# S5 head: input matrices transposed ahead of the embedding's, the skip diagonal added on TensorE, taps loaded earlier, phase tables tied to the back rotation

## The chip, the cores and the metric

The kernel runs on one core of one Trainium2 chip. The time is the device time of one execution in microseconds (us); lower is better. The core has five engines that work at once, each through its own list of instructions strictly in order: TensorE (PE, with its weight loads shown apart as PEld), VectorE (DVE), ScalarE (ACT), GpSimd (POOL) and SyncE (SP). An engine waits at an instruction until what that instruction needs is ready, and what stands behind it in the list waits too. DMA transfers are issued from the lists of SP, ACT and POOL.

## The reference

A trunk of two layers works on 1024 positions of 1024 channels. Layer 0 mixes positions with an S5 state-space mixer, layer 1 with a short gated convolution. After each mixer come a dense SwiGLU network and a per-layer embedding that is gated by the residual; at the end stands one norm. Only the S5 mixer and the embedding's product matter here:

```
for i in range(DEPTH):
    hn = rmsnorm(h, norm_mix_g[i])
    mix = s5_mixer(hn, ...) if i % 2 == 0 else shortconv_mixer(hn, ...)
    h = h + mix
    h = h + swiglu_ffn(rmsnorm(h, norm_ffn_g[i]), ffn_w_in[i], ffn_w_out[i])
    gate = sigmoid(rmsnorm(h, norm_ple_g[i]) @ ple_w_gate[i])
    h = h + gate * (p[i] @ ple_w_up[i])

# s5_mixer, per group g of 16 channels (64 groups, 64 complex states each)
abar = exp(dt * a);  bb = (abar - 1) / a * b
state[t] = abar * state[t-1] + bb @ u[t]
y[t] = real(c @ state[t]) + d_skip * u[t]
z = gelu(y);  val, gate = split(z @ w_glu);  mix = val * sigmoid(gate)
```

## The kernel before

**S5.** The 64 groups are worked on in 8 lumps of 8 groups. A position is split into a block (128 blocks) and a place inside the block (8 places, `T`). Inside a block the recurrence is a small matrix: powers of `abar` times B and C give a kernel matrix `kp` (16 rows for each group, 8 lags of 16 channels), which DMAs spread into the block-Toeplitz matrix `M`. Across blocks the recurrence is a scan on VectorE. The state is turned by a phase table `E` first, so that the scan is real, and turned back after it.

One lump `b` goes through these steps, named as in the code:

- `gen_in(b)`: ScalarE writes the normed input into `raw`, TensorE transposes it, ScalarE copies it to `U`. B times powers is built on VectorE in `raw`, transposed, and copied by ScalarE to `wbt`.
- `states(b)`: eight matmuls `pb<-U,wbt` give the block states in PSUM (`pb`, one buffer).
- `phases(k)`: VectorE builds the phase table `ptab` (one buffer) of lumps 2k and 2k+1, by doubling, in 26 instructions. `gen_phase(b)` spreads one lump's part into `E` by four DMAs that stand in POOL's list (two buffers of `E`).
- `scan_turned(b)`: VectorE's `tmp<-pb,sgnA,E`. This is the first instruction of a lump's scan; it needs all of `pb` and of `E`. The result goes by two SP DMAs with halves swapped to `tw`.
- `scan_plain(b)`, `scan_run(b)`, `scan_back(b)`: the rest of the rotation, the scan into `gv`, the back rotation in place. The last instruction of the back rotation is kept as `done["back"]`.
- `gen_out(b)`: C times powers on VectorE (`W1`), then eight matmuls `pstr<-W,bbA` to PSUM, copied by ScalarE to `kp`. Then POOL multiplies the identity by the skip weights (`dd`) and adds it to the lag-0 part of `kp` (L1190).
- `gen_swap(b)`, `gen_toeplitz(b)`: SP DMAs that build the swapped C matrix and `M` from `kp`. For the last lump both go into rooms of `ulow`, which the embedding's split weights held before.
- `outputs(b)`, `channels(b)`: matmuls with `M`, `W1`, `W2`, GELU to `zt`, transposes, split into high and low parts.

**The embedding's product.** For each layer `l`, `up_split(l)` transposes `p` and copies the weight rows `wraw` through TensorE (a matmul with the identity) into two-part form in `ulow`, and `up_product(l)` makes 96 matmuls into `pstu`. Every six of these make one tile that ScalarE copies to `ev` (two buffers) and SP stores. Nothing needs the products before a layer's network has ended, so the 192 matmuls are spread between the S5's on TensorE, layer 0's first.

**What sets the order.** The program is written in the order of the calls; a scheduler with a timing model then sets each engine's list. It follows priorities (the embedding's copies rank ahead of and its matmuls behind the rest), the free buffers of the pools (three PSUM buffers `tr` for `pstr`, two `tu` for `pstu`, one `tx` for `pstx`), and explicit marks: `tc.issue_after(x)` lets nothing inside it be placed before instruction `x`. In the kernel before, `up_split(0)` is placed after the transposes of the S5's parameters (`turned`), and the convolution's taps `cw` (three DMAs in POOL's list) are placed after the clearing of `M` (`done["clear"]`).

After the S5 come the GLU's products from `glu` on, and then networks, convolution and norms, in the same order in both kernels but for small exchanges at the network's starts.

Of the kernel before, what the change touches and what calls it, by code (L numbers as in the profile page):

```python
# [9 lines left out]
F32 = mybir.dt.float32  # L10
# [4 lines left out]
ALU = mybir.AluOpType  # L15
# [3 lines left out]
P = 128  # L19
# [5 lines left out]
def trunk(  # L25
# [7 lines left out]
    nc = tc.nc  # L33
    V, A, G, PE = nc.vector, nc.scalar, nc.gpsimd, nc.tensor

    S, D = x.shape[1], x.shape[2]
    T = S // P
# [4 lines left out]
    PKT = PD // P  # L42
    NG, NP = s5_a_re.shape[1], s5_a_re.shape[2]
    KG = D // NG
# [12 lines left out]
    ident = const.tile([P, P], F32, name="ident")  # L57
# [32 lines left out]
    def split(hi, lo, src):  # L90
        A.copy(hi, src)  # L91
        V.tensor_tensor(lo, src, hi.bitcast(F32), ALU.subtract)  # L92
# [162 lines left out]
    done = {}  # L255
# [490 lines left out]
    def up_room(l, i, s):  # L746

        return ulow[:, i, l * 2 * D + s * D:l * 2 * D + (s + 1) * D]

    def up_split(l, raws):  # L750

        for b in range(2):
            sl = slice(b * 512, (b + 1) * 512)
            for kt in range(PKT):
                pt = psum(tr)
                transposes(pt, [raws[b][:, c, kt * P:(kt + 1) * P] for c in range(4)])
                split_pe(up_room(l, kt, 0)[:, sl], up_room(l, kt, 1)[:, sl], pt)
            for kt in range(PKT):
                pt = psum(tr)
                PE.matmul(pt, ident, raws[2 + kt][:, sl], start=True, stop=True)  # L760
                split_pe(up_room(l, PKT + kt, 0)[:, sl], up_room(l, PKT + kt, 1)[:, sl], pt)

    def up_product(l, mm_prio, ev_prio):
        for t in range(T):
            sl = slice(t * P, (t + 1) * P)
            for nb in range(2):
                cs = slice(nb * 512, (nb + 1) * 512)
                with tc.high_priority(offset=mm_prio):
                    ps = psum(tu)
                    for kt in range(PKT):  # L770
                        mm3(ps, up_room(l, kt, 0)[:, sl], up_room(l, kt, 1)[:, sl], up_room(l, PKT + kt, 0)[:, cs],
                            up_room(l, PKT + kt, 1)[:, cs], kt == 0, kt == PKT - 1)
                with tc.high_priority(offset=ev_prio):
                    ev = evp.tile([P, 512], F32, name="ev", tag="ev")
                    A.copy(ev, ps)
                    nc.sync.dma_start(out=updram[l][:, t, cs], in_=ev)
# [77 lines left out]
    GB = P // KG  # L854
    NBT = NG // GB
# [11 lines left out]
    gen = tc.alloc_tile_pool(name="s5g", bufs=1, side="right")  # L867
# [38 lines left out]


    ld_n = st.tile([NG, 1], F32, name="ld_n")
    nc.scalar.dma_start(out=ld_n, in_=s5_log_dt[0].unsqueeze(1))
    an = [st.tile([NG, 2, NP], F32, name=f"an{i}") for i in range(2)]  # L910
    for i, src in enumerate((s5_a_re, s5_a_im)):
        for r in range(2):
# [1 line left out]
    gn = st.tile([NG, KG], F32, name="gn")  # L914
# [3 lines left out]
    bn = st.tile([NG, 2, NP, KG], F32, name="bn")  # L918
    for r, src in enumerate((s5_b_re, s5_b_im)):
        nc.sync.dma_start(out=bn[:, r], in_=src[0])  # L920
    raws0 = up_load(0, (rawp, rawp, gen, gen), ("r0", "r1", "wbt", "tw"))
# [16 lines left out]
    turned = PE.transpose(pp[:, 2 * NG:3 * NG], dtb, ident[:NG, :NG]).ins  # L938
    are, aim, dt = (st.tile([P, NG], F32, name=f"prm{i}") for i in range(3))
    for i, tl in enumerate((are, aim, dt)):  # L940
        V.tensor_copy(tl, pp[:, i * NG:(i + 1) * NG])
    with tc.issue_after(turned):
        up_split(0, raws0)
    up_product(0, -1, -100)


    def swapped(dst, src, queue=nc.sync):
        for a, c in ((R0, R1), (R1, R0)):
            queue.dma_start(out=dst[a], in_=src[c])

    xbs = [st.tile([P, NG, KG], F32, name=f"xb{i}") for i in range(2)]
    cA, cS = (gen.tile([P, NG, KG], F32, name=f"cc{i}") for i in range(2))
    for hf in range(2):
        pt = psum(tr)
        for k in range(8):
            PE.transpose(pt[:, k * NG:(k + 1) * NG],
                         bn.rearrange("p a n k -> p (a n) k")[:, :, 8 * hf + k], ident[:NG, :NG])
        A.copy(xbs[0][:, :, 8 * hf:8 * hf + 8], pt.rearrange("p (k g) -> p g k", k=8))
    swapped(xbs[1], xbs[0], nc.scalar)
    for hf in range(2):  # L960
        pt = psum(tr)
        for b in range(4):
            PE.transpose(pt[:, b * P:(b + 1) * P], cn[:, 4 * hf + b].rearrange("p a n -> p (a n)"), ident)
        A.activation(cA[:, 32 * hf:32 * hf + 32].rearrange("p g k -> p (g k)"), pt, AF.Copy, scale=sgnA)
    swapped(cS, cA)

    gnb = st.tile([NG, T, KG], F32, name="gnb")
    G.tensor_copy(gnb, gn.unsqueeze(1).broadcast_to([NG, T, KG]))
    gk = gen.tile([P, NG], F32, name="gk")
    pg_ = psum(tr)  # L970
    PE.transpose(pg_[:, 0:NG], gnb.rearrange("p a n -> p (a n)"), ident[:NG, :NG])
# [1 line left out]
    dk = gen.tile([KG, NG], F32, name="dk")  # L973
# [134 lines left out]
    LB = 2  # L1108
    LQ = LB * HQ
    M = run.tile([P, GB, P], F32, name="M")  # L1110
    sv = run.tile([P, GB, P], F32, name="sv")
    gv = run.tile([P, GB, P], F32, name="gv")
    done["clear"] = G.memset(M, 0.0).ins
    G.memset(gv[:, :, 0:1], 0.0)

    def tmp_tile():
# [2 lines left out]
    def phases(lump):  # L1119
        pt = gen.tile([P, 2, LQ, NJ], F32, name="ptab", tag="ptab")  # L1120
        qs = slice(lump * LQ, (lump + 1) * LQ)
        V.memset(pt[:, 0, :, 0:1], 1.0)
        V.memset(pt[:, 1, :, 0:1], 0.0)
        for k in range(6):
            n = lo = 1 << k
            shp = [P, LQ, n]
            eb, fb = (ew[:, i, qs, k:k + 1].broadcast_to(shp) for i in range(2))
            v = gen.tile([P, LQ * NJ], F32, name="ph", tag="ph")[:, 0:2 * LQ * n]
            v = v.rearrange("p (i q n) -> p i q n", i=2, q=LQ)
            u = pt[:, :, :, lo:lo + n]  # L1130
            for o, w in ((v, fb), (u, eb)):
                tt(o, pt[:, :, :, 0:n], w.unsqueeze(1).broadcast_to([P, 2, LQ, n]), ALU.mult)
            tt(u[:, 0], u[:, 0], v[:, 1], ALU.subtract)
            tt(u[:, 1], u[:, 1], v[:, 0], ALU.add)
        ptabs[lump] = pt
# [4 lines left out]
    def gen_in(b):  # L1140
# [20 lines left out]
        for hf in range(2):  # L1161
# [4 lines left out]
                              start=i == 0, stop=i == 1, is_transpose=True)  # L1166
            A.copy(wbt[:, 4 * hf:4 * hf + 4].rearrange("p c n -> p (c n)"), pt)

    def gen_out(b):

        gsl = slice(b * GB, (b + 1) * GB)
        shp = [P, GB, NL, KG]
        W1 = Ws[b] = run.tile(shp, F32, name="W1", tag="W1", bufs=2)
        A.copy(W1[:, :, 0, :], cA[:, gsl])
        shp1 = [P, GB, T, KG]
        tm = tmp_tile()[:, 0:GB * P].rearrange("p (g s k) -> p g s k", g=GB, s=T)
        for o, pw, cc in ((W1[:, :, 1:NL, :], pwr, cA), (tm, pwn, cS)):
            tt(o, pw[:, gsl, 1:NL].unsqueeze(3).broadcast_to(shp1), cc[:, gsl].unsqueeze(2).broadcast_to(shp1), ALU.mult)
        tt(W1[:, :, 1:NL, :], W1[:, :, 1:NL, :], tm, ALU.subtract)
        kp = kps[b] = gen.tile([KG, GB, T, KG], F32, name="kp", tag="kp")  # L1180
        for hf in range(2):
            pk = psum(tr)
            for c in range(4):
                PE.matmul(pk[0:KG, c * P:(c + 1) * P], bbA[:, b * GB + 4 * hf + c, :], W1[:, 4 * hf + c, 0:T, :],
                          start=True, stop=True)
            A.copy(kp[:, 4 * hf:4 * hf + 4].rearrange("p g s k -> p (g s k)"), pk[0:KG, :])
        dd = gen.tile([KG, GB, KG], F32, name="dd", tag="dd")
        G.tensor_tensor(dd, ident[:KG, :KG].unsqueeze(1).broadcast_to([KG, GB, KG]),
                        dk[:, gsl].unsqueeze(2).broadcast_to([KG, GB, KG]), ALU.mult)
        G.tensor_tensor(kp[:, :, 0, :], kp[:, :, 0, :], dd, ALU.add)  # L1190

    def halves(a):
        return [a[:, hf * 4:hf * 4 + 4] for hf in range(2)]
# [82 lines left out]
    def channels(b, zt):  # L1276
        for hf in range(2):
# [2 lines left out]
            v = ulow.rearrange("p q (k l w j) -> p q k l w j", k=KT, l=2, w=2)  # L1280
            split_pe(v[:, :, b, 0, hf, :], v[:, :, b, 1, hf, :], pt, by_kt)

    phases(0)
    gen_in(0)
    states(0)
# [10 lines left out]
    for b in range(NBT):  # L1296
        nx, after = b + 1, b + 2
        if nx < NBT:
            gen_out(nx)
        scan_run(b)  # L1300
        if nx < NBT:
            scan_turned(nx)
        if nx == last:
            late = late_halves(0)
            for part in late:
                G.memset(part, 0.0)
            gen_swap(last, late_halves(2))
            gen_toeplitz(last, late)
        scan_back(b)
        if nx < NBT:  # L1310
            scan_plain(nx)
        if nx < last:
            phase = after % LB == 0
            if phase:
                phases(after // LB)
            zt = outputs(b)
            gen_swap(nx)
            gen_toeplitz(nx, [M])
            gen_phase(after)
            gen_in(after)  # L1320
            states(after)
            if after == last:
                glu_raws.extend(glu_load(0, u) for u in range(3))
            channels(b, zt)
        else:
            zt = outputs(b)
            if nx == last:
                channels(b, zt)
# [142 lines left out]
```

## Time and profile before

| what | value |
|---|---|
| median of the runs | 2272.39 us (3 runs, 2271.51 to 2277.5) |
| the profiled execution | 2272.43 us, span 2270.6 us |
| TensorE busy | 2174.3 us (96%) |
| VectorE busy | 1644.2 us (72%) |
| ScalarE busy | 914.3 us (40%) |
| GpSimd busy | 368.3 us (16%) |
| first scan instruction of lumps 0 to 7 | 60.63, 81.46, 102.17, 121.65, 140.90, 164.68, 183.06, 201.75 us |
| first matmul of the GLU's products | 228.44 us |

Times inside the execution are microseconds from the start of the span. A row of the timeline has the start, the duration of the run of like instructions, the engine, the line, the operation, output and inputs with their sizes, how many instructions, and in brackets how long the engine had been idle and what ended that. Fp32 matmuls appear as two records each. The part of the kernel that the change touches ends where the GLU's products start.

### The profile page before, as it was taken

The numbers are of one execution on the slowest core, as the hardware profiler recorded it, in microseconds if no ns is written. First come the engines' busy times: TensorE is split into PE (matmuls) and PEld (weight loads), VectorE is DVE, ScalarE is ACT, GpSimd is POOL, SyncE is SP. The second block draws the span as 40 slices with busy tenths as digits, with TensorE's granted clock in tenths as the row PEclk, the third lists the DMA queues.
The fourth block names the chain that finished last, engine by engine and source line by source line (L and its number), as shares of the span: only waits on it lengthen the run. The fifth ranks groups of instructions, "written<-read, shape, count | busy, mean of one in ns | idle before, by whom it ended". The sixth has DMA issues, their size and how long they took to land. (4 is left out here: it accounts for less than half of the span.)

```text
span 2270.6 us, 27968 instructions
## 1 busy us (share of the span) xinstructions
PE 2174.3 (96%) x10025; PEld 1788.0 (79%) x10025; DVE 1644.2 (72%) x2742; ACT 914.3 (40%) x1743; POOL 368.3 (16%) x441
## 2 busy tenths in 40 slices
PE   7977999899999999999979999989999999999998
PEld 5866888788888877878858888868888888787887
DVE  6786424977777787887587776398777777778864
ACT  7553422544444443344343332154444344333342
POOL 2121000011111112342010000110111111224310
PEclk9999999999999999999989999999999999999999
DMA  8635301344444468664232233633444545876613
GB/s 258 181 84 126 120 19 47 103 164 147 153 148 154 144 236 306 250 233 178 90 111 85 86 96 125 253 112 121 147 160 143 164 139 187 326 258 229 253 63 112
DMA packets 234186, 358.14 MB, mean 158 GB/s; under 512 B 23856, under 2 KB 166192, under 8 KB 234048
## 3 DMA queue, kind: packets, MB, share of 16 engines
q1 hardware_dynamic: 203056, 246.72, 33.3%
q0 software_dynamic: 30432, 109.08, 13.7%
q8 instruction: 79, 1.29, 0.2%
q10 hardware_dynamic: 560, 0.57, 0.1%
q14 instruction: 59, 0.48, 0.1%
HBM read 225.53 MB, written 114.29 MB: 150 GB/s over the span
## 5 line engine op out<-in xcount | busy, mean ns | idle before, releaser
L125 PE MATMUL psmm<-ulow,ws 128*128 128x512 f32 x896 | 353.0, 394 | 14.5 <-ACT ws L91 13.1
L127 PE MATMUL psmm<-ulow,ws 128*128 128x512 f32 x896 | 351.8, 393 | 3.2 <-DVE ws L92 3.2
L126 PE MATMUL psmm<-ulow,ws 128*128 128x512 f32 x896 | 352.5, 393 | 0.4 <-DVE ulow L92 0.4
L125 PE MATMUL psmm<-uhigh,ws 128*128 128x512 f32 x672 | 262.2, 390 | 2.9 <-DVE u L370 2.9
L127 PE MATMUL psmm<-uhigh,ws 128*128 128x512 f32 x672 | 261.8, 390 | 0.0
L126 PE MATMUL psmm<-uhigh,ws 128*128 128x512 f32 x672 | 261.8, 390 | 0.0
L91 ACT CAST ws<-raw 128x512 fp32r<-128x512 f32 x224 | 138.7, 623 | 275.0 <-PE psmm L127 265.6
L488 POOL DMA_DIRECT2D hw<-hs x154 | 116.0, 754 | 765.9 <-DVE hs L92 740.0
L125 PEld LDWEIGHTS psmm<-ulow,ws 128*128 128x128 f32 x896 | 170.2, 190 | 52.1 <-ACT ws L91 14.2
L127 PEld LDWEIGHTS psmm<-ulow,ws 128*128 128x128 f32 x896 | 169.9, 190 | 39.6 <-DVE ws L92 4.3
L126 PEld LDWEIGHTS psmm<-ulow,ws 128*128 128x128 f32 x896 | 170.3, 190 | 36.0 <-DVE ulow L92 0.7
L630 DVE TENSOR_TENSOR h<-psmm,h 128x512 f32<-128x512 f32 x234 | 155.4, 682 | 45.7 <-PE psmm L127 25.8
L639 POOL TENSOR_TENSOR h<-part,h 128x512 f32<-128x512 f32 x100 | 138.9, 1393 | 243.3 <-ACT part L638 215.1
L125 PE MATMUL psmm<-ulow,w 128*128 128x512 f32 x380 | 151.1, 398 | 14.0 <-DVE h L630 10.1
L92 DVE TENSOR_TENSOR ws<-raw,ws 128x512 fp32r<-128x512 f32 x224 | 153.6, 688 | 5.7 <-ACT ws L91 5.5
L125 PEld LDWEIGHTS psmm<-uhigh,ws 128*128 128x128 f32 x672 | 126.3, 188 | 29.9 <-issue 2.8
L126 PE MATMUL psmm<-ulow,w 128*128 128x512 f32 x380 | 148.4, 390 | 0.0
L127 PE MATMUL psmm<-ulow,w 128*128 128x512 f32 x380 | 148.3, 390 | 0.0
L127 PEld LDWEIGHTS psmm<-uhigh,ws 128*128 128x128 f32 x672 | 126.2, 188 | 26.2
L126 PEld LDWEIGHTS psmm<-uhigh,ws 128*128 128x128 f32 x672 | 126.2, 188 | 26.1
L91 ACT CAST ws<-st 128x512 fp32r<-128x512 f32 x168 | 103.8, 619 | 100.9 <-PE psmm L127 91.1
L125 PE MATMUL psmm<-w,ulow 128*128 128x512 f32 (+1 forms) x360 | 139.2, 387 | 0.0
(276 smaller groups left out, 4458.7 us busy)
## 6 DMA issues: line engine op xcount, KB each, us to landing
hw<-hs POOLq DMA_DIRECT2D x154, 512.0 KB, 4.2
w<-hw SPq DMA_DIRECT2D x88, 768.0 KB, 5.5
raw<-in_ffn_w_in_dram SPq DMA_DIRECT2D x88, 512.0 KB, 3.9
raw<-in_ffn_w_out_dram SPq DMA_DIRECT2D x44, 512.0 KB, 5.5
hd<-h POOLq DMA_DIRECT2D x24, 512.0 KB, 2.9
h<-hd SPq DMA_DIRECT2D x24, 512.0 KB, 5.8
raw<-in_conv_w_in_dram SPq DMA_DIRECT2D x24, 512.0 KB, 3.8
w<-hw SPq DMA_DIRECT2D x88, 128.0 KB, 5.4
```

Source lines behind the costliest of these rows:

```text
L91: A.copy(hi, src)
L92: V.tensor_tensor(lo, src, hi.bitcast(F32), ALU.subtract)
L125: PE.matmul(ps, ahi, bhi, start=start, stop=False, skip_group_check=more)
L126: PE.matmul(ps, ahi, blo, start=False, stop=False, skip_group_check=more)
L127: PE.matmul(ps, alo, bhi, start=False, stop=stop, skip_group_check=more)
L488: nc.gpsimd.dma_start(out=hidden[j][:, :, c].rearrange("q p l j -> p q l j"), in_=hs.bitcast(F32))
L630: done["sum"] = V.tensor_tensor(h[t][:, cs], ps, h[t][:, cs], ALU.add).ins
L639: G.tensor_tensor(h[t][:, cs], part, h[t][:, cs], ALU.add)
```

## The change

1. The load of the time steps (`ld_n`) goes from ScalarE's list to SP's.
2. The sixteen transposes of the S5's input matrices (`bn`), the two copies of them to `xb`, and the two DMAs that make the swapped copy stand ahead of `up_split(0)` and `up_product(0)`, which are now placed after the last of these transposes and after the last copy.
3. In `up_split(1)`, the part for layer 1, the weight rows are split straight from SBUF, by one ScalarE copy and one VectorE subtraction of 128 x 1024 for each of the two row blocks. The four matmuls with the identity, the four with the negated identity and the eight ScalarE copies of 512 columns behind them go.
4. The taps' DMAs are placed after the copy `gnb`, an early POOL instruction, where they waited for the clearing of `M`.
5. The skip diagonal `dd` of lump b+1 is made by POOL when lump b's output matrices are made, and is added by TensorE: eight matmuls of 16 columns per lump into the same PSUM tile. POOL's addition on `kp` goes.
6. `phases` of lumps 2, 4 and 6 is placed after the latest back rotation.

```
-            for kt in range(PKT):
+        for kt in range(PKT):
+            if l:
+                split(up_room(l, PKT + kt, 0), up_room(l, PKT + kt, 1), raws[2 + kt])
+                continue
+            for b in range(2):
+                sl = slice(b * 512, (b + 1) * 512)
                 pt = psum(tr)
                 PE.matmul(pt, ident, raws[2 + kt][:, sl], start=True, stop=True)
...
-    nc.scalar.dma_start(out=ld_n, in_=s5_log_dt[0].unsqueeze(1))
+    nc.sync.dma_start(out=ld_n, in_=s5_log_dt[0].unsqueeze(1))
...
-    with tc.issue_after(turned):
-        up_split(0, raws0)
-    up_product(0, -1, -100)
...
-            PE.transpose(pt[:, k * NG:(k + 1) * NG],
-                         bn.rearrange("p a n k -> p (a n) k")[:, :, 8 * hf + k], ident[:NG, :NG])
-        A.copy(xbs[0][:, :, 8 * hf:8 * hf + 8], pt.rearrange("p (k g) -> p g k", k=8))
+            turned = PE.transpose(pt[:, k * NG:(k + 1) * NG],
+                         bn.rearrange("p a n k -> p (a n) k")[:, :, 8 * hf + k], ident[:NG, :NG]).ins
+        done["xb"] = A.copy(xbs[0][:, :, 8 * hf:8 * hf + 8], pt.rearrange("p (k g) -> p g k", k=8)).ins
     swapped(xbs[1], xbs[0], nc.scalar)
+    with tc.issue_after(turned), tc.issue_after(done["xb"]):
+        up_split(0, raws0)
+    up_product(0, -1, -100)
...
-    G.tensor_copy(gnb, gn.unsqueeze(1).broadcast_to([NG, T, KG]))
+    done["clear"] = G.tensor_copy(gnb, gn.unsqueeze(1).broadcast_to([NG, T, KG])).ins
...
-    done["clear"] = G.memset(M, 0.0).ins
+    G.memset(M, 0.0)
...
+    dds = {}
+
+    def skip(b):
+        dds[b] = gen.tile([KG, GB, KG], F32, name="dd", tag="dd")
+        G.tensor_tensor(dds[b], ident[:KG, :KG].unsqueeze(1).broadcast_to([KG, GB, KG]),
+                        dk[:, b * GB:(b + 1) * GB].unsqueeze(2).broadcast_to([KG, GB, KG]), ALU.mult)
...
                 PE.matmul(pk[0:KG, c * P:(c + 1) * P], bbA[:, b * GB + 4 * hf + c, :], W1[:, 4 * hf + c, 0:T, :],
-                          start=True, stop=True)
+                          start=c == 0, stop=True, skip_group_check=c > 0)
+            for c in range(4):
+                PE.matmul(pk[0:KG, c * P:c * P + KG], ident[:KG, :KG], dds[b][:, 4 * hf + c, :], start=False, stop=True,
+                          skip_group_check=True)
             A.copy(kp[:, 4 * hf:4 * hf + 4].rearrange("p g s k -> p (g s k)"), pk[0:KG, :])
-        dd = gen.tile([KG, GB, KG], F32, name="dd", tag="dd")
-        G.tensor_tensor(dd, ident[:KG, :KG].unsqueeze(1).broadcast_to([KG, GB, KG]),
-                        dk[:, gsl].unsqueeze(2).broadcast_to([KG, GB, KG]), ALU.mult)
-        G.tensor_tensor(kp[:, :, 0, :], kp[:, :, 0, :], dd, ALU.add)
+        if b + 1 < NBT:
+            skip(b + 1)
...
+    skip(0)
     phases(0)
...
             if phase:
-                phases(after // LB)
+                with tc.issue_after(done["back"]):
+                    phases(after // LB)
```


The edits make the scheduler set other lists. Three places follow. The first is the head of TensorE's list; `praw` is the embedding's `p`, `bn` the S5's input matrices. Before:

```order
L937 MATMUL pstr<-ident,an_138 128x64
L937 MATMUL pstr<-ident,an_139 128x64
L938 MATMUL pstr<-ident,dtb 128x64
L287 MATMUL pstr<-ident,praw 128x128 x8
L293 MATMUL pstr<-ulow,identn 128x512 x2
L760 MATMUL pstr<-wraw,ident 128x512 x2
```

In the change:

```order
L942 MATMUL pstr<-ident,an_138 128x64
L942 MATMUL pstr<-ident,an_139 128x64
L943 MATMUL pstr<-ident,dtb 128x64
L958 MATMUL pstr<-ident,bn 128x64 x16
L287 MATMUL pstr<-ident,praw 128x128 x12
L293 MATMUL pstr<-ulow,identn 128x512 x3
```

The sixteen transposes of `bn` stand ahead of the embedding's first. The product's matmuls also stand elsewhere in TensorE's list. Ahead of lump 0's last `pb` matmul there were 78 of them and are now 48; between the last `pb` of lumps 0 and 1 there are 54 in both; between those of lumps 1 and 2 there were 39 and are 36; between those of lumps 2 and 3 there were 21 and are 48; the last 6 come behind that, where before none were left.

The second place is VectorE's list just ahead of lump 2's first scan instruction. Here `W_1288` is the `W1` buffer, `ptab` and `ph` belong to `phases(1)`. Before:

```order
L882 TENSOR_TENSOR sv<-sv,tw 128x8x127
L1251 SCALAR_TENSOR_TENSOR gv<-r_132,sv 128x127 x7
L882 TENSOR_TENSOR W_1288<-pwr,cc_424 128x8x128
L1251 SCALAR_TENSOR_TENSOR gv<-r_132,sv 128x127
L882 TENSOR_TENSOR W_1288<-W_1288,tmp 128x8x128
L886 SCALAR_TENSOR_TENSOR tmp<-pb,sgnA,E 128x8x63
```

In the change:

```order
L887 TENSOR_TENSOR W_1288<-W_1288,tmp 128x8x128
L887 TENSOR_TENSOR ptab<-ptab,ph 128x8x4 x2
L887 TENSOR_TENSOR ph<-ptab,ew 128x128
L887 TENSOR_TENSOR ptab<-ptab,ew 128x16x8
L887 TENSOR_TENSOR ptab<-ptab,ph 128x8x8 x2
L887 TENSOR_TENSOR ph<-ptab,ew 128x256
L887 TENSOR_TENSOR ptab<-ptab,ew 128x16x16
L887 TENSOR_TENSOR ptab<-ptab,ph 128x8x16 x2
L887 TENSOR_TENSOR ph<-ptab,ew 128x512
L887 TENSOR_TENSOR ptab<-ptab,ew 128x16x32
L887 TENSOR_TENSOR ptab<-ptab,ph 128x8x32 x2
L891 SCALAR_TENSOR_TENSOR tmp<-pb,sgnA,E 128x8x63
```

The large steps of `phases(1)`, which stood ahead of lump 0's scan, now end directly ahead of the scan instruction that reads the table's copy `E`. The same holds at lumps 4 and 6 for `phases(2)` and `phases(3)`, which stood inside lumps 2 and 3, and inside lumps 4 and 5.

The third place is POOL's list from the skip weights on. Before:

```order
L1188 TENSOR_TENSOR dd<-ident,dk 16x128
L1100 TENSOR_TENSOR rstd<-ms_627,mhalf 128x8
L1113 MEMSET M 128x1024
L1114 MEMSET gv 128x8
L1222 DMA E<-ptab 64x2x256 x8
L818 DMA cw<-in_conv_w_dram 128x8x1 x3
L1190 TENSOR_TENSOR kp<-kp,dd 16x8x16
L1188 TENSOR_TENSOR dd<-ident,dk 16x128
```

In the change:

```order
L823 DMA cw<-in_conv_w_dram 128x8x1 x3
L1105 TENSOR_TENSOR rstd<-ms_627,mhalf 128x8
L1178 TENSOR_TENSOR dd<-ident,dk 16x128
L1118 MEMSET M 128x1024
L1119 MEMSET gv 128x8
L1235 DMA E<-ptab 64x2x256 x8
L1178 TENSOR_TENSOR dd<-ident,dk 16x128 x2
L1269 MEMSET tmp 128x8
L1235 DMA E<-ptab 64x2x256 x4
```

The taps' DMAs stand ahead of the norm's factors `rstd` and of the first `E`, the additions on `kp` are gone, and a `dd` of the next lump stands ahead of each later pair of `E` loads.

## The prediction

> **What bounds the kernel now.** I read the page's slices first, then the stretches between the first scan instructions of the lumps, then VectorE's, GpSimd's and TensorE's timelines inside them.
>
> ```profile
> span 2270.6 us, 27968 instructions
> PE   7977999899999999999979999989999999999998
> ```
>
> One slice is 56.8 us, each digit the busy tenths. From the fifth on, TensorE is busy nine tenths or more nearly everywhere, and the change leaves its order there alone but for small exchanges. A gain or loss before the GLU (228.44 us) therefore arrives at the end about one for one; I allow 1 us either way. The first four slices hold everything that changes. By lump (each stretch runs from one lump's first scan instruction to the next; the last ends at the GLU's first matmul):
>
> ```profile
> core 0: us, PE busy (x) PEld busy (x) DVE busy (x) ACT busy (x) POOL busy (x), PEclk, DMA share, GB/s
> 0.00:60.63 60.63, 48.26 (x217) 33.22 (x218) 41.21 (x200) 44.28 (x101) 11.70 (x22) 1.00 0.81 255
> 60.63:81.46 20.83, 20.83 (x128) 17.27 (x127) 13.16 (x22) 10.20 (x26) 0.84 (x2) 1.00 0.58 162
> 81.46:102.17 20.71, 20.66 (x141) 18.29 (x140) 14.79 (x22) 13.23 (x32) 3.96 (x8) 1.00 0.61 165
> 102.17:121.65 19.48, 18.54 (x137) 16.27 (x136) 18.83 (x44) 12.07 (x31) 5.06 (x9) 1.00 0.60 169
> 121.65:140.90 19.25, 14.38 (x116) 12.55 (x115) 16.78 (x27) 10.06 (x27) 4.03 (x7) 1.00 0.47 102
> 140.90:164.68 23.78, 16.83 (x115) 15.04 (x114) 18.43 (x45) 10.06 (x27) 8.12 (x7) 0.87 0.41 85
> 164.68:183.06 18.38, 14.81 (x109) 13.68 (x108) 16.37 (x27) 10.15 (x27) 3.40 (x7) 0.89 0.39 90
> 183.06:201.75 18.69, 16.19 (x132) 13.85 (x129) 14.49 (x23) 8.79 (x21) 7.44 (x7) 1.00 0.60 134
> 201.75:228.44 26.69, 18.14 (x119) 15.04 (x117) 11.55 (x22) 7.66 (x14) 1.13 (x3) 0.94 0.53 133
> ```
>
> I number the stretches 0 to 8. Stretches 1 and 2 are TensorE's: it is busy throughout, with the product's matmuls as the part that could stand elsewhere. From 3 on VectorE is the busier one and its list is the path:
>
> ```profile
> 60.63 0.74 DVE L886 SCALAR_TENSOR_TENSOR tmp<-pb,sgnA,E 128x504 f32<-128x504 f32 x1 [1.39 <-PE pb L1228]
> 81.46 0.74 DVE L886 SCALAR_TENSOR_TENSOR tmp<-pb,sgnA,E 128x504 f32<-128x504 f32 x1 [6.38 <-PE pb L1228]
> 102.17 0.74 DVE L886 SCALAR_TENSOR_TENSOR tmp<-pb,sgnA,E 128x504 f32<-128x504 f32 x1 [5.69 <-issue]
> 157.79 0.07 DVE L1122 MEMSET ptab<- 128x8 f32 x1 [4.95 <-DMA E<-ptab]
> 201.75 0.74 DVE L886 SCALAR_TENSOR_TENSOR tmp<-pb,sgnA,E 128x504 f32<-128x504 f32 x1 [3.50 <-DMA E<-ptab]
> ```
>
> VectorE waits 1.39 and 6.38 us for `pb` at lumps 0 and 1. Two later waits, 4.95 and 3.50 us, are for loads of `E`. They trace back to POOL:
>
> ```profile
> 145.62 5.22 POOL L1190 TENSOR_TENSOR kp<-kp,dd 16x128 f32<-16x128 f32 x1 [6.86 <-ACT kp L1186]
> 151.51 2.40 POOL L1222 DMA_DIRECT2D E<-ptab  x4 [0.20 <-issue]
> 174.22 2.40 POOL L1222 DMA_DIRECT2D E<-ptab  x4 [5.62 <-DVE ptab L882]
> 188.46 4.53 POOL L1190 TENSOR_TENSOR kp<-kp,dd 16x128 f32<-16x128 f32 x1 [6.11 <-ACT kp L1186]
> 193.67 2.40 POOL L1222 DMA_DIRECT2D E<-ptab  x4 [0.20 <-issue]
> ```
>
> The addition of the diagonal stands ahead of `E`(5) and `E`(7), waits 6.86 and 6.11 us for `kp`, and then runs 5.22 and 4.53 us.
>
> **The change part by part: the front.** Lump 0 starts at 60.63 because TensorE's list held 78 product matmuls ahead of `pb`; VectorE had waited only 1.39 us. The product, by lump:
>
> ```profile
> 0.00:60.63 60.63, 22.12 (x78) 13.93 (x78) 8.09 (x13) 1.00 0.81 255
> 60.63:81.46 20.83, 13.40 (x54) 9.86 (x54) 4.07 (x8) 1.00 0.58 162
> 49.22 0.58 ACT L775 COPY ev<-pstu 128x512 f32<-128x512 f32 x1 [3.51 <-DMA up<-ev]
> 34.28 0.70 ACT L1145 ACTIVATE raw<-h,rstd 128x128 f32<-128x128 f32 x2
> 56.54 0.64 ACT L1167 COPY wbt<-pstr 128x512 f32<-128x512 f32 x1
> ```
>
> One matmul costs 13.40/54 = 0.25 us in the saturated stretch, so 30 fewer are 7.4 us of TensorE ahead of lump 0. The four weight matmuls and their four companions also go. ScalarE becomes the limit here: from its first `raw` (34.28 in the trace; I take 35) its new list up to the last `wbt` holds 16 `raw` pieces, 8 `U`, 2 `W`, some 12 half-tile copies and the two new full-width copies. At the spacing before (`raw` 0.3, `U` 0.25, half tiles 0.48, full width 1.05) that is 4.9 + 2.0 + 0.5 + 5.8 + 2.1 = 15.3 us. With about 3 us of `pb` and the wait for it lump 0 starts at 53.5: **-7.1**. Bounds: 50, if no store of `ev` holds it up as the 3.51 us did; 57, if taps and inputs that now load together delay `rstd`. The earlier `xb` and taps are hidden behind this same list.
>
> **TensorE's diagonal.** The trace has no matmul of 16 columns. The nearest are:
>
> ```profile
> 24.62 1.10 PE L956 MATMUL pstr<-ident,bn 64*128 64x64 f32 x8
> 74.36 1.92 PE L1184 MATMUL pstr<-W,bbA 128*16 128x128 f32 x16
> ```
>
> A transpose of 64 columns takes 0.14; a `kp` matmul (two records) 0.24. Eight per lump lie between nothing and 1.9 us; I take 0.17 each, nearer the small one, 1.4 per lump. Stretch 1 holds two lumps' `kp`: 16 matmuls, **+2.7** (0 to 3.8). A page of the Trainium skill, TensorE: Matmul & The Clock Gate (section "Wait — 56ns, not 53.3ns?"), puts a floor of about 62 ns on a small matmul that the sequencer handles; two passes each would make 1.0 per lump, an estimate that moves the sum by under 1 us.
>
> **The phase tables.** This is the large term. Work on `ptab` in stretches 3 and 4 before:
>
> ```profile
> 102.17:121.65 19.48, 4.08 (x22) 2.40 (x4) 1.00 0.60 169
> 121.65:140.90 19.25, 2.03 (x4) 2.40 (x4) 1.00 0.47 102
> 173.17 0.75 DVE L882 TENSOR_TENSOR ptab<-ptab,ph 128x256 f32<-128x256 f32 x2
> L1222 POOL DMA_DIRECT2D E<-ptab x4: 598/604/622, 174.2 to 176.0; - x4
> DMA to landing us min/median/max: 2.3/2.7/2.8
> DMA to landing us min/median/max: 3.6/5.5/6.1
> ```
>
> One table is 4.08 + 2.03 = 6.1 us of VectorE. It was followed by other VectorE work while POOL issued `E` and the DMAs ran. Now it ends directly ahead of the scan that reads `E`, and nothing stands between. From the table's end (173.92) to POOL's first issue is 0.3 us, to its last issue 1.8 more, to landing 2.3 to 2.8 (3.6 to 6.1 for the set at 193.67): 4.8 us, up to 8.2, in which VectorE can do nothing. A lump without table and without wait for `E` takes 18.69 - 3.50 = 15.2 us (stretch 7). So a lump that ends in a table needs 15.2 + 6.1 + 4.8 = 26.1 us. TensorE would need less, so this sets stretches 2, 4 and 6: 26.1 - 20.71 = **+5.4**, 26.1 - 19.25 = **+6.9**, 26.1 - 18.38 = **+7.7**. If the 6.38 us that VectorE waited at lump 1 were the whole cover, stretch 2 would be TensorE's 20.66 + 1.4 = 22.1.
>
> **Stretch 3.** It loses the tables from VectorE but gets 48 product matmuls for 21: 18.54 + 27 x 0.25 + 1.4 = 26.7 us of TensorE. Twelve of them stand right behind `pb`(2) and run while VectorE waits for `E`(2), minus 3.0: 23.7, **+4.2** (from 0, if more of them run ahead, to +7.2).
>
> **Stretches 5 and 7** profit. The additions are gone, and `E`(5), `E`(7) follow their sisters at once, so 4.95 and 3.50 us of waiting vanish, and the table leaves stretch 5. TensorE's own work, 16.19 + 1.4 = 17.6 by stretch 7, then sets both: 17.6 - 23.78 = **-6.2** and 17.6 - 18.69 = **-1.1** (down to 15.2 each; up to 20.2, which is 23.78 - 4.95 + 1.4). This includes cold matmuls:
>
> ```profile
> 156.05 1.06 PE L1228 MATMUL pb<-U,wbt 128*128 128x128 f32 x8
> 162.50 2.08 PE L1228 MATMUL pb<-U,wbt 128*128 128x128 f32 x8
> ```
>
> The same eight records took 1.06 us and, after a pause, 2.08; the granted clock was 0.87 in that stretch. The same page of the Trainium skill (section "HAM oscillation — how this bites in real kernels") says that pauses over about 3.4 us bring on the half clock. By that rule each long wait for `E` would cost the next stretch a further 1.7 us, my estimate from the page's window; the pair above agrees in kind, and the sum would be 3.4 us higher.
>
> **The tail.** In SP's list one pair of `tw` now stands behind a GLU load and one `ulow<-W`:
>
> ```profile
> 204.99 1.19 SPq L949 DMA_DIRECT2D tw<-tmp  x2
> 212.21 1.22 DVE L882 TENSOR_TENSOR sv<-sv,tw 128x1016 f32<-128x1016 f32 x1 [5.37 <-DMA tw<-tmp]
> ```
>
> VectorE already waits 5.37 us for it, and one transfer of 3.49/4 (0.87) us more, with matmuls after longer pauses, gives **+2.0** (-1 to +3).
>
> **Sum.** -7.1 + 2.7 + 5.4 + 4.2 + 6.9 - 6.2 + 7.7 - 1.1 + 2.0 = +14.5. The profiled execution took 2272.43 us and the median is 2272.39, so no correction: 2272.4 + 14.5 = 2286.9, which I put at **2286**, a little down because stretches 3, 5 and 7 have more room below than above.
>
> **The rivals.** *TensorE runs ahead* (B). While VectorE waits for `E`, TensorE does what it can of the next stretch, so 3, 5 and 7 fall to VectorE's length: 0 for 4.2, and 15.2 for 17.6 twice, 9.0 less: 2278. For it: TensorE was busy only 14.38 and 14.81 us in stretches 4 and 6. Against it: its next matmuls need the scan's output, and only two `tu` buffers take product matmuls.
>
> *The wait is hidden* (C, the other side: faster). Tables and `E` fit into time that VectorE waits anyway, as at lumps 1 and 2 (6.38 and 5.69 us). Then stretch 2 is 22.1, and 4 and 6 are TensorE's 14.38 + 1.4 = 15.8 and 16.2: 4.0 + 10.3 + 9.9 less, so 2263. It decides once `pb` comes 10.9 us or more after VectorE reaches the table. Against it: VectorE is busy 16.78 of 19.25 us in stretch 4, and the list puts table, `E` and scan in series.
>
> *POOL is held* (D). `dd`(5) and `dd`(7) stand ahead of `E`(4) and `E`(6). Such a multiplication took 0.39 to 0.94 us:
>
> ```profile
> L1188 POOL TENSOR_TENSOR dd<-ident,dk x8: 390/438/942, 31.6 to 193.1; 16x128 f32<-16x128 f32 x8
> ```
>
> If, beside VectorE's table work, it stretches as the addition did (5.22, 4.53), the two waits grow by up to 9.8 us: 2296. Each `dd` also waits for TensorE's additions of the lump before, in the same stretch.
>
> That the change does not do what it says I see only for part 4: taps that load earlier free nobody who is late.
>
> **How the numbers follow.** My forecast gets 0.60, B 0.20, C 0.10, D 0.10. A measurement of this kernel can tell about 0.3%, 6.8 us, from no change: below 2265.6 is faster, above 2279.2 slower. C is faster: 0.10. Of B I count 0.15 as the same and 0.05 as slower; of the forecast 0.05 as the same, with front, stretch 3 and tail at their low ends together (-3.5, -4.2, -3.0), and 0.55 as slower; D is slower. Together 0.10, 0.20 and 0.70. Range: up by the front's 3.5, `E`'s 3.4 three times and 5's and 7's 2.6, seldom together, or by D: 2296. Down by B's 9 and some of the front: 2274.
>
> **What would show it.** VectorE's `tmp<-pb,sgnA,E` of lumps 2, 4 and 6 waits 4 to 8 us for `E<-ptab`, and the stretches ending there take about 26. Lump 0 starts near 53.5. The additions on `kp` are gone, and no `E` is late at lumps 5 and 7. The GLU's first matmul comes at about 242. I am wrong if the three scans wait for `pb` and not for `E`, if lump 3 starts before 121, or if the GLU starts before 235.

## The result, and the profile after

The changed kernel takes 2289.43 us (median of 4 runs, 2288.21 to 2292.14); the kernel before takes 2274.94 in the same comparison. The ratio is 1.0066, with a 95% interval of 1.0046 to 1.0086. It is slower, by 14.5 us. The forecast was 2286 with a range of 2274 to 2296.

The stretches between the lumps' first scan instructions, in the changed kernel. The columns are those of the prediction's table:

```profile
core 0: us, PE busy (x) PEld busy (x) DVE busy (x) ACT busy (x) POOL busy (x), PEclk, DMA share, GB/s
0.00:54.66 54.66, 38.49 (x171) 27.54 (x172) 39.81 (x179) 38.27 (x86) 11.97 (x22) 0.97 0.86 255
54.66:77.92 23.26, 23.26 (x165) 18.20 (x163) 10.95 (x17) 12.22 (x31) 0.84 (x3) 1.00 0.57 163
77.92:104.71 26.79, 26.23 (x184) 22.39 (x183) 19.83 (x48) 15.93 (x37) 2.85 (x6) 1.00 0.54 148
104.71:123.97 19.26, 19.26 (x138) 17.16 (x136) 14.59 (x23) 10.95 (x29) 2.52 (x5) 1.00 0.65 167
123.97:149.39 25.42, 19.93 (x170) 16.39 (x168) 20.21 (x49) 15.29 (x40) 4.69 (x9) 0.99 0.43 106
149.39:168.49 19.10, 14.20 (x96) 13.20 (x96) 14.56 (x23) 5.50 (x15) 2.47 (x5) 0.74 0.41 92
168.49:196.39 27.90, 18.68 (x166) 15.46 (x164) 20.07 (x48) 12.28 (x31) 3.31 (x7) 0.95 0.42 91
196.39:215.87 19.48, 14.58 (x96) 13.57 (x96) 14.71 (x23) 5.49 (x15) 2.47 (x5) 0.73 0.40 90
215.87:244.23 28.36, 21.59 (x141) 18.77 (x139) 11.55 (x22) 8.74 (x16) 0.71 (x2) 0.82 0.49 127
```

The long stretches are 2, 4 and 6, which end in a table; VectorE is busy for about 20 us in each, and 14.6 in the short ones. Against the forecast (length before, forecast change, measured change, all in us):

| stretch | before | forecast | measured |
|---|---|---|---|
| 0, to lump 0's scan | 60.63 | -7.1 | -5.97 |
| 1 | 20.83 | +2.7 | +2.43 |
| 2 | 20.71 | +5.4 | +6.08 |
| 3 | 19.48 | +4.2 | -0.22 |
| 4 | 19.25 | +6.9 | +6.17 |
| 5 | 23.78 | -6.2 | -4.68 |
| 6 | 18.38 | +7.7 | +9.52 |
| 7 | 18.69 | -1.1 | +0.79 |
| 8, to the GLU | 26.69 | +2.0 | +1.67 |
| sum | 228.44 | +14.5 | +15.79 |

From the GLU's first matmul to the end of the span it is 2270.6 - 228.44 = 2042.2 us before and 2286.1 - 244.23 = 2041.9 after, so in this pair what happens ahead of the GLU arrives at the end whole. The GLU starts given below come from one profiled execution each; from there to the end it was between 2039.3 and 2046.3 us in them, so GLU starts a few us apart do not rank two kernels by themselves.

VectorE's timeline of the changed kernel, the first scan instructions of lumps 2 to 6, and for lump 2 the table's last instructions ahead of it:

```profile
96.48 0.68 DVE L887 TENSOR_TENSOR ptab<-ptab,ew 128x512 f32<-128x512 f32 x1
97.20 0.76 DVE L887 TENSOR_TENSOR ptab<-ptab,ph 128x256 f32<-128x256 f32 x2
104.71 0.74 DVE L891 SCALAR_TENSOR_TENSOR tmp<-pb,sgnA,E 128x504 f32<-128x504 f32 x1 [6.75 <-DMA E<-ptab]
123.97 0.74 DVE L891 SCALAR_TENSOR_TENSOR tmp<-pb,sgnA,E 128x504 f32<-128x504 f32 x1 [4.53 <-issue]
149.39 0.74 DVE L891 SCALAR_TENSOR_TENSOR tmp<-pb,sgnA,E 128x504 f32<-128x504 f32 x1 [4.93 <-DMA E<-ptab]
168.49 0.74 DVE L891 SCALAR_TENSOR_TENSOR tmp<-pb,sgnA,E 128x504 f32<-128x504 f32 x1 [4.44 <-issue]
196.39 0.74 DVE L891 SCALAR_TENSOR_TENSOR tmp<-pb,sgnA,E 128x504 f32<-128x504 f32 x1 [7.55 <-DMA E<-ptab]
```

The scan follows the table with nothing between, and waits 6.75, 4.93 and 7.55 us for `E`: 19.2 us that the kernel before did not have there. The waits of 4.95 and 3.50 us that it had are gone. GpSimd's timeline shows where the waiting lies:

```profile
98.26 2.41 POOL L1235 DMA_DIRECT2D E<-ptab  x4 [23.60 <-DVE ptab L887]
144.75 2.40 POOL L1235 DMA_DIRECT2D E<-ptab  x4 [0.92 <-DVE ptab L887]
189.14 2.41 POOL L1235 DMA_DIRECT2D E<-ptab  x4 [0.92 <-DVE ptab L887]
```

All three sets of loads are held by the table alone (the release named in brackets). Each is issued within 2.4 us and the scan starts 4.0, 2.2 and 4.8 us after its last issue ended. At lump 4 no other transfer was issued in that time, and the four loads landed in 2.4 to 2.7 us. At lump 2 four stores of `ev`, and at lump 6 two loads of the GLU's weights, of 256 KB each, were issued beside them, and they landed in 3.8 to 4.6 and 2.5 to 5.5 us. That those transfers are the reason was not tested.

The waits are not the whole price, and the tables do not cost the same at each lump. At lump 2 the last `pb` matmuls end at 98.58, after the table's end at 97.96:

```profile
97.42 1.16 PE L1241 MATMUL pb<-U,wbt 128*128 128x128 f32 x8
```

So here VectorE would have waited for `pb` anyway, the table itself cost nothing, and the load of `E` cost the 6.1 us from 98.58 to the scan. At lumps 4 and 6 `pb` was done at 139.57 and 183.94, and the tables ended 4.9 us later each; there both the table and the load stand in the way.

TensorE pays a second time, as its timeline just behind the wait for lump 4, and two stretches of the same engine's clock, show:

```profile
151.47 1.20 PE L1283 MATMUL pstr<-W,tmp 128*128 128x128 f32 x4 [6.53 <-DVE tmp L887]
157.68 0.63 PE L1282 MATMUL pstr<-M,U 128*128 128x128 f32 x2
158.11 0.64 PE L1283 MATMUL pstr<-W,tmp 128*128 128x128 f32 x2
159.34 0.39 PE L1282 MATMUL pstr<-M,U 128*128 128x128 f32 x2
159.56 0.39 PE L1283 MATMUL pstr<-W,tmp 128*128 128x128 f32 x2
```

```profile
151.50:159.30 7.80, 5.93 (x26) 5.63 (x27) 7.70 (x10) 0.03 (x1) 2.36 (x4) 0.50 0.55 136
159.30:168.50 9.20, 8.25 (x72) 7.50 (x71) 4.76 (x11) 5.46 (x15) 0.11 (x1) 1.00 0.37 75
```

After 6.53 us without work the granted clock is 0.50 for 7.8 us, and the same pair of records takes 0.63 in place of 0.39. Such pairs start every 0.43 us before 159.34 and every 0.22 after it; the ten between 155.12 and 159.34 therefore took about 2 us longer than at full clock (my estimate from these rows). Lumps 5 and 7 then wait 4.44 and 4.43 us at their first scan instruction, although `E` for lump 5 was issued from 154.78 on; the view names no releaser ("issue"), but TensorE's last `pb` matmuls start at 167.24 and end at 168.40.

### The profile page after: what moved, and what is told of

The parts are those of the page before. It is cut to its first block, busy times and chain, and to the rows that moved or that the text cites. A ratio compares the mean times of both kernels' runs of the same rounds, so it can differ in the third digit from the quotient of the medians.

```text
span 2286.1 us, 28171 instructions
## 1 busy us (share of the span) xinstructions
PE 2182.6 (95%) x10141; PEld 1796.3 (79%) x10141; DVE 1643.3 (72%) x2744; ACT 911.1 (40%) x1737; POOL 354.8 (16%) x433
```

## The experiments

Theory: table, load of `E` and scan now stand in series, and that is the loss. Main rival: the other parts make it, by matmuls that moved behind lump 0 and by the diagonal on a busy TensorE.

**1. The whole change without part 6.**

```
             if phase:
-                with tc.issue_after(done["back"]):
-                    phases(after // LB)
+                phases(after // LB)
```

> The change without part 6: the phase tables of lumps 2, 4 and 6 are again placed by the scheduler, which puts them ahead of lumps 1 and 3 and around lump 5's first scan instruction. Theory (table, load of E and scan stand in series and cost stretches 2, 4 and 6 about 22 us, of which the front and the POOL additions that went give back some): the GLU starts near 224 to 228 us and the time is 2266 to 2272, at or under the kernel before; the waits for E at lumps 2 and 4 are gone, and one of some 5 us at lump 6 stays, where the table still ends shortly ahead of the scan. Rival (parts 2, 3 and 5, that is the product's matmuls moved behind lump 0 and the diagonal on TensorE, make the loss): it stays at 2283 to 2290.

Measured: 2271.27 us (10 runs), ratio 0.9988 (0.9977 to 1.0000). The GLU starts at 227.69. The stretches 2 to 7 of this kernel:

```profile
77.43:98.18 20.75, 20.19 (x142) 17.82 (x140) 14.56 (x23) 12.70 (x31) 2.53 (x5) 1.00 0.58 154
98.18:122.00 23.82, 23.82 (x177) 20.56 (x176) 20.32 (x48) 13.62 (x34) 7.03 (x6) 1.00 0.61 168
122.00:140.02 18.02, 17.07 (x139) 15.16 (x137) 14.49 (x23) 11.33 (x29) 3.92 (x8) 1.00 0.54 142
140.02:156.11 16.09, 14.11 (x126) 12.44 (x124) 15.82 (x35) 10.08 (x27) 2.92 (x6) 1.00 0.51 113
156.11:179.56 23.45, 19.32 (x172) 15.85 (x170) 18.40 (x38) 12.40 (x31) 3.25 (x7) 1.00 0.45 96
179.56:198.88 19.32, 14.42 (x96) 13.42 (x96) 14.71 (x22) 5.50 (x15) 2.53 (x5) 0.73 0.46 109
```

Stretches 2 and 4 fall from 26.79 and 25.42 to 20.75 and 18.02. Stretch 6, where the last table still ends ahead of the scan that reads it, stays long, and the wait of 4.98 us there is the expected one. The main rival falls: parts 1 to 5 together are not slower than the kernel before. Lumps 5 and 7 are a second pair to compare. Stretch 5, with no wait for `E` ahead of it, takes 16.09 at full clock; stretch 7, behind the wait, takes 19.32 at 0.73. (The profiled execution, 2276.11 us, is the slowest of the ten.)

**2. The kernel before with part 6 alone.**

```
             if phase:
-                phases(after // LB)
+                with tc.issue_after(done["back"]):
+                    phases(after // LB)
```

> The kernel before with part 6 alone. Theory: lumps 2, 4 and 6 wait for E as in the change, the front keeps lump 0 at 60.6, and POOL's additions stand ahead of two of the loads: GLU at 243 to 250, time 2287 to 2294, so at least as slow as the whole change. Rival (other parts make the loss): 2270 to 2277.

Measured: 2285.30 us (5 runs), ratio 1.0047 (1.0028 to 1.0065), GLU at 241.28, below the 243 to 250 and the 2287 to 2294 expected, so it is not as slow as the whole change. The waits for `E` at lumps 2, 4 and 6 are 4.99, 6.69 and 4.95 us. One line of the change makes, on the old kernel, about 11 us of its 14.5; taken out of the whole change (experiment 1) it is worth about 18, so the parts do not simply add.

**3. The kernel before with part 5 alone.** The edit is the diff's part on `skip` and `gen_out`, on the old kernel.

> The kernel before with part 5 alone (skip diagonal by TensorE). Theory: the waits of 4.95 and 3.50 us for E go, TensorE has about 0.6 us more per lump, but the scheduler now puts the end of the last table ahead of lump 6, where a wait of some 5 us comes up: 2268 to 2274, no clear difference. Rival (matmuls of 16 columns on a busy TensorE are the loss): 2277 to 2285.

Measured: 2275.73 us (10 runs), ratio 1.0009 (0.9997 to 1.0021): no clear difference, but the median lies above the 2268 to 2274 that I expected, and in the profiled execution, the slowest of the ten (2278.62), the GLU starts at 234.68, 6 us later than before. Its stretch 3 and stretch 6:

```profile
103.12:127.47 24.35, 24.35 (x184) 20.80 (x182) 20.32 (x48) 14.62 (x36) 8.10 (x8) 1.00 0.58 164
162.07:185.51 23.44, 19.33 (x172) 15.85 (x170) 18.40 (x37) 12.39 (x31) 3.25 (x7) 1.00 0.44 96
```

The new list has 36 product matmuls in stretch 3 for 21, and the last table ahead of lump 6, with a wait of 4.97 us for `E`. The 15 more matmuls, at 0.25 us each, are 3.7 us of the 4.9 that stretch 3 has grown. The small matmuls are not the larger part: `dd` takes 1.4 us of TensorE for two lumps in stretch 1 of the whole change (below).

**4. Parts 1 to 4 alone.** The change with the diffs of parts 5 and 6 undone.

> The change without parts 5 and 6, so parts 1 to 4 on the kernel before. Theory: lump 0 starts at 54 to 55; the matmuls of the product that are moved behind it take most of that back in stretches 1 to 4, and lump 6 waits for E behind table and addition: 2266 to 2273. Rival (the front's gain of 6 us arrives whole): 2265 to 2267. Rival (the moved matmuls cost more than the front gains): 2275 and more.

Measured: 2272.07 us (10 runs), ratio 0.9994 (0.9980 to 1.0008); lump 0 starts at 55.06, lump 3 at 116.77, the GLU at 228.59. The time lies in the 2266 to 2273 expected. The front's 5.6 us have shrunk to nothing by the GLU: at lump 6 there is a wait of 5.43 us for `E`, since with the new front the scheduler also splits the last table around lump 5's scan.

**5. The first kernel (that of experiment 1), with each table complete before the odd lump's scan.**

```
-            tt(u[:, 1], u[:, 1], v[:, 0], ALU.add)
+            done["table"] = V.tensor_tensor(u[:, 1], u[:, 1], v[:, 0], ALU.add).ins
...
         if nx < NBT:
-            scan_turned(nx)
+            with tc.issue_after(done["table"]) if nx % LB else ExitStack():
+                scan_turned(nx)
...
             gen_swap(nx)
+            if after % LB and after < last:
+                phases((after + 1) // LB)
```

(`phases(1)` goes ahead of `gen_in(1)`, and the call in the loop's even turns goes.)

> The first experiment's kernel with one more rule: each phase table is called one lump earlier and has to be complete before the scan of the odd lump ahead of it (lump 5's scan waits for the last table, which the list otherwise splits around it). Theory (a table costs only where it ends directly ahead of the scan that reads it): lump 5 starts some 4 us later than in the first experiment (156.1), lump 6's wait of 4.98 us and some 4.5 us of table leave stretch 6; the GLU starts near 222 to 225 us, time 2265 to 2270. Rival (the time of the table itself counts wherever it stands): the GLU stays at 227 to 228 and the time at 2271.

Measured: 2269.22 us (9 runs), ratio 0.9974 (0.9964 to 0.9984): faster than the kernel before, by 0.26%. GLU at 224.63. Its stretches 5 to 7:

```profile
140.27:161.16 20.89, 18.77 (x166) 15.37 (x164) 20.39 (x49) 12.39 (x31) 3.55 (x7) 1.00 0.45 96
161.16:179.59 18.43, 13.54 (x96) 12.54 (x96) 14.48 (x23) 7.94 (x23) 2.52 (x5) 0.81 0.42 95
179.59:195.14 15.55, 13.68 (x122) 12.08 (x121) 14.50 (x22) 7.62 (x19) 2.91 (x6) 1.00 0.65 149
```

Lump 5 starts 5.05 us later than in the first experiment and lump 6 at the same time, so up to there the table's time and the wait only changed places. Nor is the slow clock gone: with lump 5's scan held by the table, TensorE pauses 2.14 us and stretch 6 runs at 0.81. The gain comes behind it: stretch 7 takes 15.55 us in place of 19.32, without the wait and at full clock; the tail gives 0.7 of these 3.8 us back.

**6. No tables for lumps 2 to 7.** The kernel leaves them out and loads `E` from the first table, so its output is not the layer's; only its time is of use.

```
-                phases(after // LB)
+                ptabs[after // LB] = ptabs[0]
```

> The first experiment's kernel without the tables of lumps 2 to 7: their E is loaded from the first table, so 18.3 us of VectorE and every wait for a table are left out. It bounds what any placing of the tables can reach. Theory: VectorE waits in the first stretches anyway, so the GLU starts at 213 to 219 us, 9 to 15 us earlier than in the first experiment, time 2257 to 2263. Rival (TensorE bounds all stretches once E is on time): 224 or later.

Measured: 2261.57 us (2 runs), ratio 0.9941 (0.9923 to 0.9960), GLU at 217.85. The fifth experiment is within 6.8 us of this bound at the GLU (224.63), though its tables still take 18.3 us of VectorE: some 11 us of them cost nothing there (a comparison of two profiled executions).

**7 and 8. The front.** The first kernel without part 3 (the three lines `if l: ... continue` removed), and without part 2 (`up_split(0)` and `up_product(0)` back ahead of the transposes of `bn`).

> The first experiment's kernel without part 3: layer 1's weight rows go through TensorE again. The list then holds 72 product matmuls ahead of lump 0 in place of 48. Theory (30 fewer matmuls ahead of lump 0 are what brings its start forward): lump 0 starts at 59 to 62 us as in the kernel before. Rival (the earlier input matrices or taps bring it forward): 54 to 56.

> The first experiment's kernel without part 2: the transposes of the input matrices stand behind the embedding's again; part 3 stays, with 48 product matmuls ahead of lump 0. Theory: lump 0 starts at 54 to 56 us, since ScalarE's list behind the first raw piece is unchanged. Rival (the early swapped copy of the input matrices brings the start forward): 58 to 61, with VectorE waiting about 4 us for xb as in the kernel before.

Measured, one run each: without part 3 lump 0 starts at 63.28 and the GLU at 230.70 (2272.08 us). Without part 2 lump 0 starts at 53.62 and the GLU at 227.33 (2272.62 us), although VectorE waits 4.00 us for `xb` again. VectorE's timeline of the eighth:

```profile
36.59 0.74 DVE L887 TENSOR_TENSOR tb<-xb,sm 128x512 f32<-128x512 f32 x1 [4.00 <-DMA xb<-xb]
53.62 0.74 DVE L891 SCALAR_TENSOR_TENSOR tmp<-pb,sgnA,E 128x504 f32<-128x504 f32 x1 [2.56 <-PE pb L1241]
```

Without part 3 lump 0 starts later than the 59 to 62 expected and 9.1 us later than in the first experiment. Its list holds 72 product matmuls ahead of lump 0 in place of 48; the 24 more are about 6 us at 0.25 each. The rest would be the weight rows' own matmuls and copies, which part 3 removes too; the two were not tested apart. The earlier input matrices bring nothing that can be seen.

**9. The whole change with the loads of `E` on two queues.**

```
-                nc.gpsimd.dma_start(out=E[...],
+                (nc.sync if two else nc.gpsimd).dma_start(out=E[...],
```

> The whole change, with two of the four loads of each E issued by SP and two by POOL. Theory (the scan waits for issue plus landing of E): the last issue comes 1.2 us earlier, so each of the waits at lumps 2, 4 and 6 (6.75, 4.93, 7.55) shrinks by about 1.2, and the time is 2284 to 2288. Rival (the landing alone sets the wait, the loads queue behind other transfers): waits and time as in the change, 2288 to 2291.

Measured: 2287.94 us (4 runs), ratio 1.0066 (1.0044 to 1.0088), the same as the change. The waits are 6.35, 4.69 and 6.71. Of the 1.2 us expected only 0.2 to 0.8 came. POOL's two loads and SP's two, for lump 2:

```profile
98.79 1.23 POOL L1235 DMA_DIRECT2D E<-ptab  x2 [23.62 <-DVE ptab L887]
99.97 2.41 SPq L1235 DMA_DIRECT2D E<-ptab  x2
```

At lump 2 SP started its two 1.2 us later and took 2.41 for them, so the last issue ended 3.9 us behind the table, where it was 2.7 in the change; at lump 6 it was 2.7 in both. Only at lump 4 did both queues end earlier, 1.5 us behind the table in place of 2.7, and there the wait shrank least, by 0.24. So the waits do not follow the last issue, and they do not stay as they were either: neither theory holds alone.

**10. The change without part 5**, so with POOL's addition on `kp`.

> The change without part 5: POOL adds the skip diagonal again, and two such additions stand ahead of E(4) and E(6) in its list. Theory (the loss is table and load; the additions finish under the table's 6 us): waits for E of 5 to 8 us at lumps 2, 4 and 6 as in the change, GLU at 240 to 246, 2285 to 2291. Rival (an addition stretched to 5 us holds the loads): one or two waits above 9 us, GLU after 248.

Measured, one run: 2293.33 us, GLU at 248.85, waits for `E` of 7.60, 6.73 and 8.66. No wait is above 9 us, and the additions took 0.44 to 0.81 us, so none was stretched; but the rival's time came true and not the theory's, since the GLU starts 4.6 us later than in the change. GpSimd's timeline:

```profile
193.98 0.44 POOL L1200 TENSOR_TENSOR kp<-kp,dd 16x128 f32<-16x128 f32 x1 [15.14 <-ACT kp L1198]
194.50 0.39 POOL L1178 TENSOR_TENSOR dd<-ident,dk 16x128 f32<-16x128 f32 x1
195.10 2.40 POOL L1232 DMA_DIRECT2D E<-ptab  x4 [0.21 <-issue]
```

The addition waits for ScalarE's `kp`, and the loads of `E`(6) follow it. The theory had the additions done under the table, but the two ahead of `E`(4) and `E`(6) started at 147.06 and 193.98, after the tables had ended (146.18 and 193.80). What holds the loads here is the addition's place in POOL's list and what it waits for: the first load is issued 2.0 and 1.3 us behind the table in place of 0.3, and the waits are 1.8 and 1.1 longer than in the change. At lump 2 no addition stands ahead, and the wait is still 0.85 longer. Whether an addition beside the table's work would be stretched, as the rival says, this run cannot show, since neither ran beside it. In one run, then, part 5 is of use where the tables are late; alone (experiment 3) it was of none.

**11. The first kernel without part 4** (`done["clear"]` back on the clearing of `M`), **and 12, the fifth with the same edit.**

> The first experiment's kernel without part 4: the taps' DMAs stand again behind the clearing of M and the first E in POOL's list; the lists are otherwise the same. Theory (nothing late waits for the taps): lump 0 at 54 to 55 us and the GLU at 227 to 228.5. Rival (the 7.93 us that VectorE waited for a queue behind the taps come back): lump 0 at 57 or later.

> The fifth experiment's kernel (tables complete before the odd lumps) with the taps as in the kernel before (the eleventh's edit). Theory (both effects add: the fifth had the GLU at 224.6, the late taps brought lump 0 forward by some 0.8 us): GLU at 222 to 225, 2266 to 2270, ratio to the kernel before 0.995 to 0.998. Rival (the eleventh's single run was only a good one): the same as the fifth within its interval, GLU at 224 to 226.

Measured: the eleventh, one run, 2268.64 us, lump 0 at 53.39, GLU at 225.27. The twelfth, 9 runs, 2267.27 us, ratio 0.9964 (0.9950 to 0.9978), lump 0 at 53.39, lump 6 at 179.61, GLU at 224.75. Of the 7.93 us that VectorE waited behind the taps in the kernel before, 1.48 and 0.52 come back, and lump 0 even starts 0.8 to 1.0 us earlier with late taps; but in the twelfth this is used up by lump 6, and its interval overlaps the fifth's. That late taps help is not shown. The twelfth is faster than the kernel before. The eleventh's single run lies inside the range of the kernel before (2267.24 to 2276.92 in the same comparison), so for it this is open.

## Why the prediction was right, step by step

**The phase tables** (forecast +5.4, +6.9, +7.7; measured +6.08, +6.17, +9.52). The step and its size held, and none of the named signs of being wrong came: the three scans waited for `E`, lump 3 started at 123.97 and the GLU at 244.23. Undone alone it takes 16.5 us from the GLU's start (244.23 to 227.69), and alone on the old kernel it adds 12.8 (228.44 to 241.28). The one term that was short is the wait: 4.8 us was taken, 4.93 to 7.55 measured. The loads of lumps 2 and 6 landed in up to 4.6 and 5.5 us; the rows quoted had both 2.7 and 5.5, and I took the smaller. One thing the account did not see: at lump 2 the table filled time in which VectorE would have waited for `pb`, which is the half of rival C that was right; only the load was added there.

**The front** (-7.1; -5.97). ScalarE's first `raw` came at 36.21, where I took 35, and its list up to the last `wbt` ended at 52.0, so 15.8 us for a forecast of 15.3. Experiment 7 supports the cause given, the matmuls ahead of lump 0, for about 6 of 9.1 us. The reading of which part does it was too even: part 3 does, part 2 does nothing.

**TensorE's diagonal** (+2.7; +2.43). The sum agreed but not its cause. The groups of TensorE in stretch 1 of the changed kernel:

```profile
L1196 PE MATMUL pstr<-W,bbA 128*16 128x128 f32 x32 | 4.4, 274 | 0.0
L1199 PE MATMUL pstr<-dd,ident 16*16 16x16 f32 x32 | 1.4, 173 | 0.0
```

The 16 small matmuls take 1.4 us, 0.09 each, half of the 0.17 I took. The `kp` matmuls take 4.4 where they took 3.8 before, and there are four more transposes of `raw`. The page TensorE: Matmul & The Clock Gate of the Trainium skill (section "Wait — 56ns, not 53.3ns?"), which I cited for 62 ns a pass, gives that for one way of decoding, and a floor of about 25 ns however small the matmul. Eight records in a row, from TensorE's timeline of the fifth experiment:

```profile
198.28 0.36 PE L1199 MATMUL pstr<-dd,ident 16*16 16x16 f32 x8
```

One lasts 0.17 us, so 0.19/7 = 0.027 us lie between starts, close to the floor of 25 ns and well under 62.

**Stretch 3** (+4.2; -0.22). Here rival B was right. While VectorE waited 6.75 us at lump 2, TensorE did not pause: it was busy 26.23 of stretch 2's 26.79 us. Besides the twelve product matmuls that I had counted it did lump 2's `kp` matmuls, the diagonal and the transposes there, and had 19.26 us left for stretch 3.

**Stretches 5 and 7** (-6.2, -1.1; -4.68, +0.79). The waits for `E` went as forecast, but 17.6 was too low by 1.5 and 1.9 us. TensorE had run ahead, as B says (96 records are left in each), yet at clocks of 0.74 and 0.73. I had left out of the sum the half clock after a pause, for which I had worked out an estimate of 1.7 us each from the Trainium skill's rule (same page, section "HAM oscillation — how this bites in real kernels"). Added to the sum it would have made up the 1.5 and 1.9. The pairs shown above give about 2 us for stretch 5, so the trace agrees in size. It does not agree on the length of the pause: in experiment 5 the clock was halved after a pause of 2.14 us, where the page speaks of gaps over about 3.4. Between experiments 1 and 5 stretch 7 takes 19.32 us behind a wait and 15.55 without one; these 3.8 us are more than the clock's share, since part of them is work that waited too. Rival D had no part: the `dd` ahead of `E`(4) and `E`(6) took 0.39 us beside the table's last steps and were done before the table. Rival C, as a time, falls with the three waits.

**The tail** (+2.0; +1.67). `tw` does stand behind one `ulow<-W` and VectorE waits 5.75 us for it (5.37 before). The rest of the 1.67 was not tested.

So the sum of +14.5 against +15.79 rests on two errors of about 4 us each way, 4.4 too much for stretch 3 and 3.4 too little for 5 and 7, and on 1.8 us too little for lump 6. The mechanism, table and load in series at lumps 2, 4 and 6, held; that the sum came so close is luck, since the two errors nearly cancel.

## What to carry to other kernels

A table that is loaded through a DMA has to be ready one load ahead of its reader; when a rule of order puts its making directly ahead of the reader, the load's whole latency is paid each time, here 4.9 to 7.6 us. Ask of each added order rule not what it may move out of the way but what it makes adjacent, and place the work in a wait that is there already: placed ahead of the odd lumps' scans, where VectorE waited for TensorE, the three tables cost about 7 us of the 18 that they take. A pause of several us also costs the matmul engine in what follows: the stretch behind a wait was 3 to 4 us longer here, of which about 2 are the slower clock.

## What had not been expected of the hardware

A fp32 matmul of 16 columns and 16 rows came at 0.027 us from record to record, where a 128-column one takes about 0.11. After a pause of 6.53 us the clock was granted at 0.50 for 7.8 us, longer than the pause, and in experiment 5 a pause of 2.14 us was enough to halve it. And a second DMA queue, with half of four small loads on it, shortened the waits by 0.2 to 0.8 us, the least where it brought the last issue forward by 1.2.
